# Log-sum-exp over heads: loads of two rows per partition, two heads on TensorE, hand-ordered issue and tapered last loads

## The chip, the cores and the metric

The kernel runs on one core of a Trainium2 chip. The metric is the device time of one execution in microseconds.

The time that is measured is about 1.9 us longer than the span that the profile shows (347.34 us against 345.5 us). Positions "at 331 us" below are in the span.

## The reference

```python
B, S, D, H = 8, 2048, 2048, 8            # x: (8, 2048, 2048) f32, bias: (8, 256) f32
x_heads = x.reshape(B, S, H, 256).transpose(0, 2, 1, 3) + bias[None, :, None, :]
x_tiled = np.repeat(x_heads, 2, axis=2)  # every row's result appears twice
mx  = x_tiled.max(axis=-1, keepdims=True)
lse = mx.squeeze(-1) + np.log(np.exp(x_tiled - mx).sum(axis=-1))   # (8, 8, 4096)
```

For each row and each of 8 heads, the kernel needs the log of the sum of exp(x + bias) over 256 columns. The kernels skip the maximum and compute log(sum(exp(x) * exp(bias))). The input is 134.2 MB, the output 1 MB. Each input element is read once, so the work is a stream: load, exp, weighted sum.

## The kernel before

A tile is 128 rows of 2048 columns, 1 MB, one row (8 KB) per partition. Seven heads go ScalarE (exp in place) then VectorE (multiply with exp(bias) and sum, one instruction per head, plus a second one that reads the sum out). The eighth head goes TensorE (bias row plus x by an identity matrix, in bf16) then ScalarE (exp with a sum).

```python
N_TTR_HEADS = 7
XIN_BUFS = 8
# ... constants: ident, ident_bf, ones_bf, brow (bias), w_rep = exp(bias) on 128 partitions ...
for b in range(B):
    for sblk in range(nsblk):                                   # 16 tiles per batch
        xt = xin.tile([P, D], mybir.dt.float32, name="xt")
        nc.sync.dma_start(out=xt, in_=x[b, s0 : s0 + P, :])      # 1 MB, 8 KB per partition
        for h in range(n_ttr, H):                                # the eighth head
            nc.tensor.matmul(ps, lhsT=ones_bf[0:1, :], rhs=b_hi, start=True, stop=False)
            nc.tensor.matmul(ps, lhsT=ident_bf[:, :], rhs=x_hi, start=False, stop=True)
            nc.scalar.activation(out=ps, in_=ps, func=ACT.Exp,
                                 accum_out=R[:, b, h, sblk : sblk + 1])
        nc.scalar.activation(out=xt[:, 0 : n_ttr * Dh], in_=xt[:, 0 : n_ttr * Dh], func=ACT.Exp)
        for h in range(n_ttr):                                   # seven heads
            nc.vector.tensor_tensor_reduce(out=junk, in0=xt[:, sl], in1=w_rep[:, sl],
                scale=1.0, scalar=0.0, op0=ALU.mult, op1=ALU.add,
                accum_out=R[:, b, h, sblk : sblk + 1])
    # ... per batch: transpose R (TensorE), Ln with each value written twice (ScalarE), store ...
```

The softmax here doesn't subtract the row's maximum and nothing guards it: scores larger than these inputs give would overflow.

## Time and profile before

| | before |
|---|---|
| time, median of 3 | 347.34 us (347.29 to 347.41) |
| span of the profile | 345.5 us |
| busy: VectorE / ScalarE / TensorE | 92% / 79% / 28% |
| load rate, 20 to 240 us | 421 GB/s |
| x has landed completely at | 336.71 us |
| from there to the end | 8.77 us |

The last two rows come from the trace's record of single DMA packets: 336.71 us is the end of the last packet of x, counted like every position here from the start of the profile's span. The prediction below has 336.9 us for it and 8.5 us for the rest, since it counts packets from a point 0.24 us earlier.

The page's slices of the kernel before (the span in 40 equal slices: mean busy share of the 16 DMA engines in tenths, and what they moved), and two lines of its DMA queues (packets, MB, share of 16 engines' span):

```profile
DMA  7999999999999999999999999999999999999700
GB/s 303 427 421 421 417 422 423 422 421 421 419 423 417 424 421 419 423 420 424 423 418 418 424 420 423 421 422 419 422 416 412 370 401 424 420 411 409 286 24 15
...
q1 hardware_dynamic: 18576, 134.36, 94.3%
q14 instruction: 23, 0.19, 0.1%
```

The DMA engines are busy in every slice from the 2nd to the 37th, at 409 to 427 GB/s but for a dip in slices 32 and 33 (268 to 285 us). Slice 39 (328 to 337 us) passes at 24 GB/s, about the rate of one DMA engine of 16 (the mean busy share of the 16 is 0.06 from 328 to 336 us, at 25 GB/s); the last slice holds the store of the results. Queue q14 is the fetch of instructions: 23 packets of 8 KB.

Groups of instructions of the kernel before (line, engine, operation, shapes, count | busy us, mean ns of one | idle before them and what ended it):

```profile
L131 DVE CUSTOM_DVE_ANT_0 junk<-xt,w_rep 128x256 f32<-128x256 f32 x896 | 316.3, 422 | 24.0 <-ACT xt L123 15.4
L123 ACT ACTIVATE xt<-xt 128x1792 f32<-128x1792 f32 x128 | 217.2, 1698 | 62.7 <-DMA xt<-in_x_dram 56.2
...
L112 PE MATMUL ps<-xt,ident_bf 128*128 128x256 bf16 x128 | 49.3, 385 | 21.4 <-DMA xt<-in_x_dram 21.3
L115 ACT ACTIVATE ps<-ps 128x256 f32<-128x256 f32 x128 | 47.2, 369 | 0.0
```

VectorE's 896 reductions start about 0.347 us apart (the 422 ns of one overlap the next), so 7 of them take 2.43 us. A megabyte arrives every 2.49 us at 421 GB/s. VectorE is nearly as busy as the DMA, but it is not what the others wait for, as the waits say (engine and tile <- what ended the wait: us in total, times, longest):

```profile
ACT xt L123 <- DMA xt<-in_x_dram: 56.2, 105, 3.7
DVE junk L131 <- ACT xt L123: 15.4, 23, 1.0
```

ScalarE, which with TensorE is the first to touch x, waits 105 times for x to land. Once x is there, the rest follows.

### The profile page before, as it was taken

How to read it: one execution, taken by the hardware profiler on the slowest of the kernel's cores; microseconds unless marked ns; L12 is line 12 of the kernel's file. 1: busy time of each engine (PE TensorE's matmuls, PEld its weight loads, DVE VectorE, ACT ScalarE, POOL GpSimd, SP SyncE). 2: the span in 40 equal slices, each digit the busy share in tenths (PEclk: the TensorE clock that was granted, in tenths of full speed). 3: DMA queues.
4: the chain of work that ended last, by engine and by line, in shares of the span. 5: the costliest groups of instructions: out<-in, count | busy, mean ns of one | idle time of the engine just before them, and what ended most of it. 6: DMA issues, size and time to landing. Idle time of an engine off the chain costs nothing. (4 is left out here: it accounts for less than half of the span.)

```text
span 345.5 us, 3541 instructions
## 1 busy us (share of the span) xinstructions
PE 95.0 (28%) x268; PEld 27.6 (8%) x268; DVE 316.6 (92%) x1793; ACT 272.4 (79%) x397; POOL 5.0 (1%) x15
## 2 busy tenths in 40 slices
PE   2423223223322323322332322232223232222220
PEld 0100000000000000000010000000000000000000
DVE  0899989899898998999989989899899998999985
ACT  4978878788787887878778878788777887878872
POOL 1000000000000000000000000000000000000000
DMA  7999999999999999999999999999999999999700
GB/s 303 427 421 421 417 422 423 422 421 421 419 423 417 424 421 419 423 420 424 423 418 418 424 420 423 421 422 419 422 416 412 370 401 424 420 411 409 286 24 15
DMA packets 18939, 135.50 MB, mean 392 GB/s; under 512 B 2177, under 2 KB 2305, under 8 KB 2529
## 3 DMA queue, kind: packets, MB, share of 16 engines
q1 hardware_dynamic: 18576, 134.36, 94.3%
q0 software_dynamic: 336, 0.92, 0.7%
q14 instruction: 23, 0.19, 0.1%
q8 instruction: 2, 0.03, 0.0%
q10 hardware_dynamic: 2, 0.01, 0.0%
HBM read 134.23 MB, written 1.05 MB: 392 GB/s over the span
## 5 line engine op out<-in xcount | busy, mean ns | idle before, releaser
L131 DVE CUSTOM_DVE_ANT_0 junk<-xt,w_rep 128x256 f32<-128x256 f32 x896 | 316.3, 422 | 24.0 <-ACT xt L123 15.4
L123 ACT ACTIVATE xt<-xt 128x1792 f32<-128x1792 f32 x128 | 217.2, 1698 | 62.7 <-DMA xt<-in_x_dram 56.2
L109 PE MATMUL ps<-brow,ones_bf 1*128 1x256 bf16 x128 | 46.9, 368 | 207.6 <-ACT ps L115 207.5
L131 DVE DVE_READ_ACCUMULATOR2_ANT R<- 128x1 f32 x896 | 74.8, 83 | 0.0
L112 PE MATMUL ps<-xt,ident_bf 128*128 128x256 bf16 x128 | 49.3, 385 | 21.4 <-DMA xt<-in_x_dram 21.3
L115 ACT ACTIVATE ps<-ps 128x256 f32<-128x256 f32 x128 | 47.2, 369 | 0.0
L112 PEld LDWEIGHTS <-ident_bf 128*128 128x128 bf16 x128 | 13.2, 104 | 245.2 <-issue 245.2
L115 ACT ACTIVATION_READ_ACCUMULATOR ps<-ps 128x1 f32 x128 | 23.5, 184 | 0.0
L109 PEld LDWEIGHTS <-ones_bf 1*128 1x128 bf16 x128 | 12.5, 98 | 45.6 <-issue 45.6
L152 ACT ACTIVATE res<-tps 128x256 f32<-128x256 f32 x8 | 3.1, 383 | 6.6 <-PE tps L143 6.6
L159 POOL DMA_DIRECT2D out_dram<-res x7 | 3.9, 562 | 295.9 <-ACT res L152 295.9
L143 PE MATMUL tps<-ident,R 128*128 128x128 f32 x8 | 3.6, 452 | 13.8 <-DVE R L131 13.8
L79 PE MATMUL psw<-brow,ones_bf 1*128 1x512 bf16 x4 | 2.4, 601 | 4.2 <-DMA brow<-in_bias_dram 2.4
L143 PEld LDWEIGHTS tps<-ident,R 128*128 128x128 f32 x8 | 1.4, 180 | 19.3 <-issue 15.8
L82 ACT ACTIVATE w_rep<-psw 128x512 f32<-128x512 f32 x4 | 2.3, 593 | 0.0
L50 ACT ACT_TABLE_LOAD x1 | 1.3, 1283 | 0.7 <-PEq L174 0.7
L63 DVE MEMSET ones_bf<- 1x128 bf16 x1 | 0.2, 165 | 0.8 <-PEq L174 0.8
L79 PEld LDWEIGHTS <-ones_bf 1*128 1x128 bf16 x4 | 0.5, 118 | 4.0 <-issue 3.0
masks.py:199 POOL TENSOR_SCALAR_AFFINE_SELECT ident<-ident 128x128 f32<-128x128 f32 x1 | 0.3, 285 | 0.0
masks.py:199 POOL TENSOR_SCALAR_AFFINE_SELECT ident_bf<-ident_bf 128x128 bf16<-128x128 bf16 x1 | 0.3, 285 | 0.0
masks.py:197 POOL MEMSET ident<- 128x128 f32 x1 | 0.2, 205 | 0.3 <-POOLq L174 0.3
masks.py:197 POOL MEMSET ident_bf<- 128x128 bf16 x1 | 0.2, 206 | 0.0
(4 smaller groups left out, 0.4 us busy)
## 6 DMA issues: line engine op xcount, KB each, us to landing
xt<-in_x_dram SPq DMA_DIRECT2D x128, 1024.0 KB, 16.4
out_dram<-res POOLq DMA_DIRECT2D x7, 128.0 KB, 5.8
out_dram<-res SPq DMA_DIRECT2D x1, 128.0 KB
brow<-in_bias_dram ACTq DMA_DIRECT2D x1, 8.0 KB
```

The lines of the kernel that those rows point to most:

```text
L50: nc.scalar.add_instruction(mybir.InstLoadActFuncSet(name=nc.get_next_instruction_name(), act_func_set_id=set_idx,))
L63: nc.vector.memset(ones_bf, 1.0)
L79: nc.tensor.matmul(psw, lhsT=ones_bf[0:1, :], rhs=b_hi_c, start=True, stop=True)
L82: nc.scalar.activation(out=w_rep[:, c * WCH : (c + 1) * WCH], in_=psw, func=ACT.Exp)
L109: nc.tensor.matmul(ps, lhsT=ones_bf[0:1, :], rhs=b_hi, start=True, stop=False)
L112: nc.tensor.matmul(ps, lhsT=ident_bf[:, :], rhs=x_hi, start=False, stop=True)
L115: nc.scalar.activation(out=ps, in_=ps, func=ACT.Exp, accum_out=R[:, b, h, sblk : sblk + 1],)
L123: nc.scalar.activation(out=xt[:, 0 : n_ttr * Dh], in_=xt[:, 0 : n_ttr * Dh], func=ACT.Exp,)
L131: nc.vector.tensor_tensor_reduce(out=junk, in0=xt[:, sl], in1=w_rep[:, sl], scale=1.0, scalar=0.0, op0=ALU.mult, op1=ALU.add, accum_out=R[ ...
L143: nc.tensor.transpose(out=ps, in_=R[:, b].rearrange("p h s -> p (h s)"), identity=ident)
L152: nc.scalar.activation(out=res, in_=ps_view, func=ACT.Ln)
L159: out_eng.dma_start(out=ov, in_=res.rearrange("p s e -> p (s e)"))
```

## The change

The change has four parts, and each has its own aim.

1. **2 MB loads, two rows per partition.** Each partition gets 16 KB in one piece, in place of 8 KB.
2. **Fixed buffers and hand-ordered issue.** Nine buffers of 2 MB and an order of issue written out by hand replace pools and a scheduler.
3. **Two heads by TensorE and ScalarE.** VectorE falls from 14 reductions per 2 MB to 12. The matmuls are fp32 now, so x is no longer cut to bf16 for these heads; the bias goes in as three bf16 parts.
4. **Tapering.** The last nine tiles come in pieces of 1 MB, then 0.5 MB, then down to 256 columns, so that little work is left when the last byte lands. The last tile has its own small result path.

```diff
-N_TTR_HEADS = 7
-XIN_BUFS = 8
+K = 2
+NPE = 2
+NBUF = 9
+LAST_CUTS = [[0, 1024, 2048], [0, 512, 1024, 1536, 1792, 2048]]
...
+    xts = [sb.tile([P, K, D], F32, name=f"xt{i}") for i in range(NBUF)]
+    def pieces(t):
+        left = T - 1 - t
+        if left > 8:
+            return [(0, K, 0, D)]
+        if left > 3:
+            return [(k, k + 1, 0, D) for k in range(K)]
+        cuts = [[0, D // 2, D]] * K if left else LAST_CUTS
+        return [(k, k + 1, c0, c1) for k in range(K) for c0, c1 in zip(cuts[k], cuts[k][1:])]
+    def rows_of(t):
+        if t < T - 1:
+            return v.rearrange("(p k) d -> p k d", k=K)
+        return v.rearrange("(k p) d -> p k d", k=K)
+    order = tc.manual_schedule()
...
-                nc.tensor.matmul(ps, lhsT=ident_bf[:, :], rhs=x_hi, start=False, stop=True)
+            nc.tensor.matmul(p[:, 0:CPE], lhsT=ident, rhs=v, start=False, stop=True)   # fp32, 512 columns
...
+        for k0, k1, c0, c1 in pieces(t):
+            if c0 == 0:
+                got = add_bias([xt[:, k, 0:CPE] for k in range(k0, k1)])   # TensorE
+            exp_inplace(xt[:, k0:k1, w0:c1])                               # ScalarE
+            if c0 == 0:
+                for k in range(k0, k1):
+                    sum_biased(got[k - k0], lambda h: sum_at(k, h))        # ScalarE, 2 heads
+            for k in range(k0, k1):
+                for c in range(w0, c1, Dh):
+                    weigh(xt[:, k, c : c + Dh], c // Dh, sum_at(k, c // Dh))   # VectorE
+            if last and k0 == K - 1 and c0 == 0:
+                finish(b, ..., NBLK - 1, K, 0, 1, [nc.sync])     # Ln and 8 stores of the earlier blocks
+        if t + NBUF < T:
+            load(t + NBUF)
```

## The prediction

> **What bounds it now.** The loads. In the page's slices the DMA engines run at 417 to 427 GB/s nearly throughout; 134.2 MB of x at 421 GB/s is 319 us of the 345.5 us span. The waits agree: ScalarE waits 56 us, 105 times, for x to land, about 0.4 us per tile. VectorE is close behind: 7 reductions per tile start 0.347 us apart, 2.43 us of the 2.49 that 1 MB takes. The DMA queue waits for free buffers (259 us), but with 16.4 us of loads already queued: no starvation.
>
> **The end.** The DMA packet records show 15 engines finishing x at 326 to 327 us and one at 336.9; the slices fall to 24 GB/s, one engine's rate. I put the lag down to instruction fetch: 23 packets of 8 KB, most beside an x packet that took about 0.97 us instead of 0.31. After the last landing 8.5 us follow: exp 1.7, seven reductions, transpose 0.45, Ln 0.39, store and completion 3.
>
> **What the change does, per 2 MB (4.98 us today).**
> - VectorE: 12 reductions instead of 14, 4.16 us instead of 4.86.
> - ScalarE: one exp of 3072 (estimated from 1792 in 1.70 us: 2.7) plus four sums of 256 at 0.395, 4.3 us instead of 4.0; still below the DMA.
> - TensorE: two fp32 matmuls of 512 columns. The fp32 transpose of 128 takes 0.45 us, bf16 512 columns 0.60, so I estimate 1.9 us each; with the bias matmuls 4.3 to 5 us at today's speed.
> - Loads: 16 KB contiguous per partition, so packets should become 16 KB. Now 8 KB takes 309 ns at best (306 apart), 311 on average; [...] Halving the packets saves an estimated 2.5 to 5 ns per 8 KB, 2.5 to 5 us over 1024 packets per engine: 424 to 428 GB/s.
> - 18 MB of buffers instead of 8, fixed order: almost nothing, since the DMA does not starve.
> - Fetch lag: VectorE and TensorE instructions fall, ScalarE's rise from about 400 to 1120; I count 24 fetches instead of 23. The lag of 10 us stays and limits the gain.
> - Tail: the last piece is 256 columns, exp 0.3 and one reduction. But in-order ScalarE first waits for a 1.9 us matmul, then does Ln of earlier blocks and other pieces: I estimate 7.3 us instead of 8.5.
>
> **Sum.** On the critical path: load stream -4, tail -1.2, lag +0.4. Relieving VectorE is off it. 347.3 - 4.8 = 342.5 us, range 337.5 to 346.5. Faster by over 2%: 0.27; within: 0.70; slower: 0.03.
>
> **What would show it right.** x packets of 16 KB at 605 to 615 ns; steady slices of 424 to 428 GB/s; VectorE and ScalarE 80 to 87% busy, ScalarE's main wait still x landing; a last stretch of about 10 us at one engine's rate; last landing to end about 7.3 us.
>
> **What would make it wrong.** Packets stay 8 KB or bring no rate: 346. [...] The lag shrinks, or the dip at 265 to 285 us (370 and 401 GB/s) vanishes: below 338. TensorE becomes the pace: 348. The eight small stores at the end hold back the final ones: +1 to 2 us.

## The result, and the profile after

| | before | after |
|---|---|---|
| time, median | 347.35 us | 341.16 us (340.64 to 341.37, 4 runs) |
| span of the profile | 345.5 us | 339.2 us |
| busy: VectorE / ScalarE / TensorE | 92 / 79 / 28% | 80 / 87 / 70% |
| load rate, 20 to 240 us | 421 GB/s | 428 GB/s |
| last packet of x ends at | 336.71 us | 331.25 us |
| from there to the end | 8.77 us | 7.94 us |

The ratio is 0.982 (95% interval 0.9806 to 0.9834): within 2%. A ratio here is the mean time of one kernel's runs over that of the other's runs of the same rounds, so it is not quite the ratio of the medians that are quoted. Executions over 1.5% slower than the fastest of the same kernel are left out of the means. Of the 6.3 us that the span lost, 5.5 us lie before the last landing of x and 0.8 us after it.

Slices and DMA queues of the kernel after:

```profile
PEclk9999577587876587876589877698777698595756
DMA  8999999999999999999999999999999999988950
GB/s 300 427 433 428 424 429 430 429 429 426 425 430 430 423 427 424 436 423 428 425 435 417 431 425 428 430 428 425 429 432 424 428 418 420 422 346 277 309 209 19
...
q1 hardware_dynamic: 12800, 135.27, 95.6%
q14 instruction: 20, 0.16, 0.1%
```

From the 2nd to the 35th, the slices run at 417 to 436 GB/s. Then there is something new: four slices (36 to 39, 297 to 331 us) at 346, 277, 309 and 209 GB/s. The stretch at one DMA engine's rate (about 25 GB/s) is now only 2.5 us long, from 329 to 331.5 us, in place of nine.

Groups of instructions of the kernel after:

```profile
L170 DVE CUSTOM_DVE_ANT_0 junk<-xt,w_rep 128x256 f32<-128x256 f32 x768 | 271.0, 420 | 63.4 <-ACT xt L164 63.2
L150 PE MATMUL ps<-xt,ident 128*128 128x512 f32 x256 | 188.8, 872 | 84.0 <-DMA xt<-in_x_dram 83.5
L164 ACT ACTIVATE xt<-xt 128x3072 f32<-128x3072 f32 (+4 forms) x83 | 179.4, 2172 | 20.0 <-DMA xt<-in_x_dram 17.2
L156 ACT ACTIVATE ps<-ps 128x256 f32<-128x256 f32 x256 | 94.6, 370 | 14.0 <-PE ps L150 9.2
```

TensorE's clock is now granted at 0.77 on average, and its 256 fp32 records (two to a matmul) take 0.87 us each, so 1.75 us per matmul. ScalarE took over as the busiest engine, with 609 instructions in place of 397.

Waits of the engines in the kernel after, then those of the DMA queue (SPq), two lines of the kernel before (L92) and two of the kernel after (L90):

```profile
ACT xt L164 <- DMA xt<-in_x_dram: 17.2, 32, 1.6
DVE junk L170 <- ACT xt L164: 63.2, 66, 11.2
ACT ps L156 <- PE ps L150: 9.2, 6, 6.2
```

```profile
SPq L92 <- DVE R L131: 259.3, 120, 5.8
...
SPq L92 <- DMA xt<-in_x_dram: 1.3, 1, 1.3
...
SPq L90 <- DMA xt<-in_x_dram: 153.3, 59, 5.4
SPq L90 <- DVE R L170: 111.5, 51, 7.5
```

ScalarE's main wait is still the landing of x, but it fell from 56 us to 17 us, because ScalarE has more to do between landings. VectorE waits 63 us for ScalarE. The loads still wait for VectorE to free buffers (111.5 us), but e3 below shows that VectorE's busy time does not set the pace. In the queue there is a wait that hardly existed before: a load now waits for an older load to land (153.3 us, 59 times, where it was 1.3 us, once). In the trace the loads use eight semaphores in turn, and none starts before the transfer that had its semaphore last has landed: the eighth load is issued at 8.45 us, after the first one has landed at 8.43, although its buffer is free. At most eight loads are outstanding at any time in this trace, and in the taper these eight are small.

### The profile page after: what moved, and what is told of

It reads as the page before. It is cut to its first block, busy times and chain, and to the rows that moved or that the text cites. A ratio compares the mean times of both kernels' runs of the same rounds, so it can differ in the third digit from the quotient of the medians.

```text
span 339.2 us, 3449 instructions
## 1 busy us (share of the span) xinstructions
PE 238.3 (70%) x408; PEld 70.3 (21%) x408; DVE 271.8 (80%) x1538; ACT 295.0 (87%) x609; POOL 6.3 (2%) x14
## 4 chain that ended last, share of the span: by engine, by line
DMA 75%; ACT 17%; PE 4%; POOL 1%; issue 1%; DVE 0%; POOLq 0%; DVEq 0%; SPq 0%; ACTq 0%
DMA xt<-in_x_dram 72%; ACT xt L164 10%; ACT ps L156 6%; PE ps L150 3%; DMA b<-bparts 2%; DMA brow<-in_bias_dram 1%; PE ps L145 1%; ACT res L199 0%; DVE junk L170 0%; POOL brest L117 0%; POOL brest L119 0%; POOL bparts L116 0%; POOL bparts L118 0%; POOL b L122 0%; POOL bparts L120 0%
## 5 line engine op out<-in xcount | busy, mean ns | idle before, releaser
L170 DVE CUSTOM_DVE_ANT_0 junk<-xt,w_rep 128x256 f32<-128x256 f32 x768 | 271.0, 420 | 63.4 <-ACT xt L164 63.2
L150 PE MATMUL ps<-xt,ident 128*128 128x512 f32 x256 | 188.8, 872 | 84.0 <-DMA xt<-in_x_dram 83.5
L164 ACT ACTIVATE xt<-xt 128x3072 f32<-128x3072 f32 (+4 forms) x83 | 179.4, 2172 | 20.0 <-DMA xt<-in_x_dram 17.2
L156 ACT ACTIVATE ps<-ps 128x256 f32<-128x256 f32 x256 | 94.6, 370 | 14.0 <-PE ps L150 9.2
L150 PEld LDWEIGHTS ps<-xt,ident 128*128 128x128 f32 x256 | 58.0, 254 | 164.5 <-DMA xt<-in_x_dram 119.5
L170 DVE DVE_READ_ACCUMULATOR2_ANT R<- 128x1 f32 x756 | 61.9, 82 | 0.0
L145 PE MATMUL ps<-b,ones 3*128 3x512 bf16 x128 | 47.0, 439 | 6.5 <-DMA b<-bparts 6.5
L156 ACT ACTIVATION_READ_ACCUMULATOR ps<-ps 128x1 f32 x256 | 48.7, 190 | 0.0
L145 PEld LDWEIGHTS <-ones 3*128 3x128 bf16 x128 | 7.9, 95 | 83.1 <-issue 75.1
L126 PE MATMUL ps<-brow,ones 1*128 1x512 f32 x6 | 5.5, 1078 | 3.6 <-DMA brow<-in_bias_dram 3.6
```

What stands on the lines that cost most here:

```text
L126: nc.tensor.matmul(ps[i], lhsT=ones, rhs=brow[:, CPE + c : CPE + c + MM], start=True, stop=True,)
L145: nc.tensor.matmul(p[:, 0:CPE], lhsT=ones3, rhs=b3, start=True, stop=False)
L150: nc.tensor.matmul(p[:, 0:CPE], lhsT=ident, rhs=v, start=False, stop=True)
L156: nc.scalar.activation(out=p[:, c : c + Dh], in_=p[:, c : c + Dh], func=ACT.Exp, accum_out=dst(h),)
L164: nc.scalar.activation(out=v, in_=v, func=ACT.Exp)
L170: nc.vector.tensor_tensor_reduce(out=j, in0=v, in1=w_rep[:, c : c + Dh], scale=1.0, scalar=0.0, op0=ALU.mult, op1=ALU.add, accum_out=dst,)
```

## The experiments

Twelve kernels were run. In the table, "last x" is the end of the last packet of x in that run's profile, "rest" is from there to the end of the span.

| run | time, us | ratio to before | last x | rest |
|---|---|---|---|---|
| before | 347.3 | 1 | 336.71 | 8.77 |
| after | 341.16 | 0.982 | 331.25 | 7.94 |
| e1_8k_packets | 345.57 | 0.9954 | 335.42 | 7.80 |
| e2_pool_1024 | 341.45 | 0.9833 | 331.63 | 7.85 |
| e3_one_head_pe | 342.42 | 0.986 | 332.36 | 8.37 |
| e4_three_tiles_15 | 376.25 | 1.0818 | 364.94 | 7.75 |
| e5_pool_3072 | 462.7 | 1.3323 | 331.49 | 129 |
| e6_half_the_reductions | 335.03 | 0.9642 | 325.62 | 7.83 |
| e7_no_taper | 342.49 | 0.9864 | 329.32 | 11.55 |
| e8_before_16k_packets | 345.29 | 0.9942 | 332.30 | 11.19 |
| e9_before_16_bufs | 347.45 | 1.0004 | 336.84 | 8.76 |
| e10_half_red_pool_2048 | 339.6 | 0.9777 | 329.92 | 7.80 |
| e11_tail | 339.34 | 0.979 | 329.87 | 7.28 |
| e12_tail_32k_packets | 339.08 | 0.975 | 328.42 | 8.89 |

### e1: the change with packets of 8 KB

```diff
-        if t < T - 1:
-            return v.rearrange("(p k) d -> p k d", k=K)
         return v.rearrange("(k p) d -> p k d", k=K)
```

The place of a result in the output tile was swapped to match, so the result stays right.

> The changed kernel with the row order of its last tile used for all tiles: still 2 MB per load, but each partition gets two separate 8 KB rows, so packets are 8 KB as before; everything else stays. Theory A (packet size carries the load-stream part): steady slices fall from about 427.5 to about 421.5 GB/s, 4.4 us over 134.2 MB, so the time is about 345.5 us. Rival B (buffers, fixed order or 2 MB loads carry it): packets of 8 KB change nothing, about 341 us.

Measured: 345.57 us, and the last landing 4.17 us later. The steady stretch (windows of the run: stretch in us, its length, busy time and count of each engine, granted clock, DMA share, GB/s) is back at 421; the second line is the same stretch of the kernel after:

```profile
20.00:240.00 220.00, 163.34 (x274) 47.18 (x272) 183.66 (x1041) 198.41 (x400) 0.00 (x0) 0.72 1.01 421
```

```profile
20.00:240.00 220.00, 158.47 (x278) 47.62 (x277) 186.44 (x1056) 200.89 (x406) 0.00 (x0) 0.76 1.01 428
```

Theory A holds to within 0.1 us. The packet size, not the size of the load, the buffers or the order, carries 4.4 of the 6.2 us.

### e8: the same part alone, in the kernel before

```diff
-XIN_BUFS = 8
+XIN_BUFS = 6
...
-            xt = xin.tile([P, D], mybir.dt.float32, name="xt")
-            nc.sync.dma_start(out=xt, in_=x[b, s0 : s0 + P, :])
+            if k2 == 0:
+                xt2 = xin.tile([P, 2, D], mybir.dt.float32, name="xt2")
+                nc.sync.dma_start(out=xt2,
+                    in_=x[b, s0 : s0 + 2 * P, :].rearrange("(p k) d -> p k d", k=2))
+            xt = xt2[:, k2, :]
```

> The kernel before with one part of the change alone: loads of 2 MB, two consecutive rows per partition (16 KB packets), six buffers of 2 MB in place of eight of 1 MB; rows of the output come out permuted on purpose. Theory A (packet size is worth 4.4 us): about 343 us, steady slices near 427 GB/s. If the freeing of buffers in steps of 2 MB throttled the loads, it would be slower than that. Rival (fixed order and relieved VectorE are needed for the gain): 347 us.

Measured: 345.29 us. The stream gains what it should, since the last landing is 4.41 us earlier at 428 GB/s. But the rest after it grows by 2.42 us, to 11.19 us: the last load is 2 MB, so two tiles' worth of work is left when it lands, not one. More than half of the gain is given back at the end. This is what the tapering is for.

### e7: the change without tapering

```diff
-        if left > 8:
+        if left > 0:
             return [(0, K, 0, D)]
-        if left > 3: ... cuts ...
+        return [(k, k + 1, 0, D) for k in range(K)]
```

> The changed kernel with every load of 2 MB but the last two rows' (1 MB each), so no tapering. Estimate: the last landing comes about 0.9 us earlier (no packets under 8 KB), but ScalarE has up to 2 MB of work (4.4 us) queued when the last megabyte lands, so the stretch from last landing to end grows from 7.7 to 10 us or more: time about 343 us. Rival (tapering is worth nothing): 340.3 us.

Measured: 342.49 us. The last landing comes 1.93 us earlier, the rest grows by 3.61 us. Tapering costs stream time and gives more than that back at the end: 1.3 us net. Its packets are 8, 4, 2 and 1 KB, but how much of the 1.93 us these explain was not separated. The expectation had both signs right and both sizes too small.

### e3: one head on TensorE instead of two

```diff
-NPE = 2
+NPE = 1
```

> The changed kernel with one head on TensorE and ScalarE instead of two, so VectorE does 14 reductions per 2 MB again (4.86 us). Prediction's claim A (relieving VectorE is off the critical path): time near 341 us, plus about 1 us for 2 VectorE fetches more and 2 fewer elsewhere; at most 343. Rival B (VectorE's relief is what made the kernel faster): back to about 346 us, with VectorE near 93% busy and few waits for ScalarE.

Measured: 342.42 us, with VectorE 92% busy, exactly as in the kernel before. Relieving VectorE's arithmetic is therefore worth 1.3 us at most, and not because VectorE was the pace: the last landing itself moved by 1.11 us. The runs below explain that movement.

### e9: more buffers in the kernel before

```diff
-XIN_BUFS = 8
+XIN_BUFS = 16
```

> The kernel before with 16 buffers of 1 MB in place of 8 and nothing else changed. Prediction's claim (buffers are worth almost nothing; the dips of the slices after 260 us are only the fast DMA engines waiting for the late one): dips later or gone, time 346.5 to 347.4 us. Rival (lack of buffers starves the loads): 344 us or less.

Measured: 347.45 us, no change. But the dip at slices 32 and 33 is gone:

```profile
GB/s 305 429 419 423 422 421 424 417 424 420 421 423 417 423 422 417 425 421 420 425 418 424 421 421 419 422 424 422 421 421 420 419 423 422 421 419 422 168 24 15
```

So the dip never cost anything. Most DMA engines were ahead of one (in the kernel before, 15 are done with x at 326 to 327 us, the last at 336.71) and ran out of free buffers; with more buffers they run further ahead and then are done earlier (slice 38 passes at 168 GB/s in place of 286). The last landing (336.84 us) is set by the late engine, which does not care. In this run the loads no longer wait for VectorE to free buffers (259.3 us before) but for older loads to land (234.3 us, 110 times), so more than the eight outstanding loads seen in the trace of the kernel after were probably not tried. The same reading applies to the four low slices after the change: the other engines wait there, while the late one works on.

### e2: 1024 more instructions on GpSimd

Why is one DMA engine late? The prediction put it down to instruction fetch. In the trace of the kernel after, fetch packets are followed by a slow packet of x, and the records fall into two kinds:

```
                     fetch at us, took ns -> next x packet, took ns (a normal 16 KB packet: 611)
VectorE-like         53.81, 325 -> 1273    76.82, 325 -> 1273    153.13, 325 -> 1273   (12 in the run)
others               40.62, 309 ->  989    108.91, 318 -> 989    170.45, 309 ->  987
```

The first kind comes every 22 to 29 us, in which VectorE's records number 107 to 140, 127 on average; this is why it is called VectorE-like. It holds its DMA engine for about 0.31 + (1.27 - 0.61) = 0.97 us. In the kernel before, a single engine still moves x after 328 us, and the fetch at 332.12 us, 22.8 us after the last one of this kind, is followed on it by an x packet of 891 ns in place of 309: this kind does fall on the late engine.

```diff
+        for _ in range(16):
+            nc.gpsimd.memset(tiny, 0.0)      # [1, 1], once per tile x 16
```

> The changed kernel plus 1024 one-element memsets on the idle GpSimd, 16 per tile, which nothing waits for: 8 more instruction fetches of 8 KB. Theory A (one DMA engine carries all instruction fetches and sets the last landing; a fetch costs it 0.66 to 1 us): fetch packets rise from 20 to about 28 and the time by 5 to 8 us, to about 347 us, with a longer end at one engine's rate. Rival B (the late engine is late for another reason, or the fetches spread over the 16 engines): time within 1 us of 341.2.

Measured: 341.45 us, with the last landing 0.38 us later, although the fetches rose from 20 to 28:

```profile
q14 instruction: 28, 0.23, 0.2%
```

Theory A as it was put fell: a fetch is not a fetch. Either fetches do not matter at all, or they are spread over the 16 engines, or GpSimd's go through another DMA engine than VectorE's. The last is theory A2: each compute engine's instructions come through a DMA engine of its own, and the one that serves VectorE is the late one, because VectorE has the most instructions (1627 records in the kernel after, ScalarE 696).

### e5: 3072 more instructions on GpSimd

The same edit with 48 memsets per tile.

> As the run with 1024 more GpSimd memsets, but with 3072 (48 per tile), so about 24 more fetches of 8 KB, more than VectorE's 12. That earlier run cost only 0.3 us for 8 fetches. Theory A2 (each compute engine's instructions are fetched through one DMA engine of its own; VectorE's is the late one, so GpSimd's fetches cost nothing until they outnumber VectorE's): GpSimd's DMA engine becomes the late one with about 25 fetches at 0.6 to 0.7 us, time 5 to 9 us longer, about 348 us. Rival B (fetches are not what makes one engine late): within 1.5 us of 341.3.

Measured: 462.7 us, but this decides nothing. The one-element memsets follow each other every 0.147 us (each is 89 ns long), so GpSimd alone needed 450 us for 3072 of them, and only 17 of its fetches came before the last landing, which stayed at 331.49 us. The run does give GpSimd's fetch a size: fetch packets of mostly 309 ns, each followed by an x packet of about 960 ns, so 0.31 + 0.35 = 0.66 us. Seventeen of these are 11.2 us, and VectorE's twelve at 0.97 us are 11.6 us. Under A2 nothing should have moved, so the experiment was too small for its own question.

### e6: half of VectorE's instructions for the same data

```diff
-                for c in range(w0, c1, Dh):
-                    weigh(xt[:, k, c : c + Dh], c // Dh, sum_at(k, c // Dh))
+                for c in range(w0, c1, 2 * Dh):
+                    e = min(c + 2 * Dh, c1)
+                    weigh(xt[:, k, c:e], c // Dh, sum_at(k, c // Dh))
```

The result is wrong: two heads are summed into one. (Not shown: a scratch tile twice as wide, and nine one-time presets of the result tiles on GpSimd.)

> The changed kernel with one VectorE reduction over 512 columns in place of two over 256: the same data, half the VectorE instructions (6 fetches fewer), on purpose a wrong result. Theory A (VectorE's fetches make one DMA engine late and set the last landing): last landing 3.5 to 5 us earlier, time about 337 us. Rival B: VectorE's busy time falls by at most a tenth and is not critical, so about 341 us.

Measured: 335.03 us, 6.1 us less, with the last landing 5.63 us earlier. Slices, the fetch queue and a group of this run:

```profile
GB/s 302 425 436 432 425 428 427 423 432 428 424 428 427 430 427 429 427 430 425 430 426 429 425 427 434 429 429 421 432 425 432 425 418 422 422 419 410 398 171 18
...
q14 instruction: 14, 0.11, 0.1%
...
L173 DVE CUSTOM_DVE_ANT_0 junk<-xt,w_rep 128x512 f32<-128x512 f32 x385 | 240.9, 686 | 87.6 <-ACT xt L166 79.9
```

VectorE is still busy with its reductions for 241 us (271 us before the edit), the steady rate is the same, and fetches fell from 20 to 14. Six fetches at 0.97 us would be 5.8 us. And the low slices near the end nearly vanish (419, 410, 398), which fits the reading that those engines had been waiting for the late one.

### e10: the same, with 2048 more instructions on GpSimd

```diff
+        for _ in range(32):
+            nc.gpsimd.memset(tiny, 0.0)
```

> The run with half the VectorE reductions (6 VectorE fetches, 335.0 us) plus 2048 one-element GpSimd memsets (16 more fetches, all before the last landing, since a memset takes 0.146 us and they end near 300 us). In the earlier traces a VectorE fetch held its DMA engine 0.97 us, a GpSimd one 0.66 us. Theory A2 (each compute engine has a DMA engine of its own for its fetches): GpSimd's becomes the late one, 16 x 0.66 = 10.6 against 5.8 us, so the last landing comes about 4.7 us later than at half the reductions, time about 339.5 us. Theory A1 (all fetches go through the same DMA engine): 10.6 us later, 345.6 us. Rival B (GpSimd's fetches do not hold up x at all): 335 us.

The fetch queue of this run (14 packets in e6):

```profile
q14 instruction: 31, 0.25, 0.2%
```

Measured: 339.6 us, against 339.5 expected under A2, 345.6 under A1 and 335 under B; the last landing moved by 4.30 us (4.7 expected). With VectorE's instructions halved, GpSimd's own fetches become the ones that set the end. This is what a DMA engine per compute engine predicts, and neither rival predicts it. Nor does a spread over the 16 engines: one fetch more on each would be about 0.66 us.

The trace does not record which of the 16 engines moved a packet, but its records let one infer it. A packet starts 3 or 4 ns before its predecessor on the same engine ends, and a 2 MB load is 8 packets and one of 4 bytes on each engine, so a search can join the packets into 16 chains. In e10, from 14 to 275 us, all 14 GpSimd fetches fall on one chain, the one that had moved least of x (412.5 times 16 KB), and all 5 of VectorE's kind on another (420); the rest had 421.5 to 427.5. In the kernel after, from 27 to 270 us, all 10 fetches of VectorE's kind fall on one chain, again the last (380.5, the others 393.5 to 397.5). In e2, e5 and e6 the search splits VectorE's kind over two chains (in e5 GpSimd's too), but no chain of e2 or e5 holds fetches of both; the packets of e8, e11 and the kernel before could not be joined cleanly.

### e4: sparing one DMA engine

```diff
+        if t in (14, 30, 46):
+            for p0, p1 in ((0, 120), (120, P)):
+                nc.sync.dma_start(out=xts[t % NBUF][p0:p1], in_=rows_of(t)[p0:p1])
+            return
```

The edit was meant to give one DMA engine less of x than the others. That a load split this way does so was the author's assumption, on which the figures of theories A and A' rest; no trace of this case shows it.

> The changed kernel with three of the 55 full loads (tiles 14, 30, 46) split into 120 and 8 partitions; [...] Theory A (one engine is behind by about 15 us, and it is the highest): [...] the last landing comes about 13 us earlier, time about 328 us. Theory A' (one engine, but not the highest): [...] about +1 us, 342 us. Rival B (no single engine is behind): about 341 to 342 us.

Measured: 376.25 us, the median of four runs (one of them, 380.68 us, was slow and is left out of the ratio; the fast three are 374.62 to 376.57 us). Both theories about the late engine are untouched by it, since the split loads themselves are slow. In the stretch of the second one the engines were busy and moved half as much:

```profile
160.00:170.00 10.00, 2.35 (x6) 0.61 (x6) 5.54 (x32) 4.36 (x9) 0.00 (x0) 0.75 1.01 206
```

Three such tiles cost 35 us. Why the split loads run at half rate was not found out. As a way to spare one engine it is useless.

### e11: another order in the last row

Timeline of ScalarE in the kernel after, around the last landing at 331.25 us (start us, us, engine, line, operation, tiles, count, idle before):

```profile
330.88 1.05 ACT L164 ACTIVATE xt<-xt 128x1024 f32<-128x1024 f32 x1
331.83 0.38 ACT L156 ACTIVATE ps<-ps 128x256 f32<-128x256 f32 x1
...
332.35 0.37 ACT L156 ACTIVATE ps<-ps 128x256 f32<-128x256 f32 x1
...
332.72 0.58 ACT L199 ACTIVATE res<-tps 56x512 f32<-56x512 f32 x1
333.20 1.75 ACT L164 ACTIVATE xt<-xt 128x512 f32<-128x512 f32 x4
334.85 0.36 ACT L199 ACTIVATE res<-tps 8x256 f32<-8x256 f32 x1
336.48 0.37 ACT L199 ACTIVATE res<-tps 8x256 f32<-8x256 f32 x1 [1.28 <-PE tps L186]
```

When the last piece has landed, ScalarE still does the sums of the TensorE heads, the Ln of the earlier blocks, and only then the four last exps that VectorE waits for.

```diff
-        if left > 3:
+        if left > 0:
             return [(k, k + 1, 0, D) for k in range(K)]
-            if c0 == 0:
+            late = last and k0 == K - 1
+            if c1 == D if late else c0 == 0:          # last row: the TensorE sums come last
                 ... sum_biased ...
-            if last and k0 == K - 1 and c0 == 0:
+            if late and c0 == D // 4:                 # Ln of earlier blocks after the first exp
```

> A version meant to beat both: whole rows instead of half rows in the three tiles before the last, and in the last row the exps go first, then the Ln of the earlier blocks, the TensorE sums last (a third result buffer, so that the last store need not wait). If ScalarE's in-order queue after the last landing is what the tail consists of: last landing about 0.4 us earlier, the stretch after it about 1.8 us shorter, time 339 us. If the tail is set elsewhere (stores, VectorE): 341 us.

Measured: 339.34 us (338.93 to 340.96, ratio 0.979, interval 0.9769 to 0.981, which overlaps that of the change). The last landing came 1.38 us earlier, more than expected; the half-row loads are gone, which is probably why. The rest shrank by 0.66 us where 1.8 was expected: ScalarE was busy without a gap from well before the last landing to 333.7 us, so reordering moves its work about but removes none of it. A small gain, not clearly told from none.

### e12: packets of 32 KB

If 8 KB packets take 313.9 ns and 16 KB packets 307.75 ns per 8 KB (means of the records of 20 to 240 us), and a packet costs a fixed time beside its bytes, that time is 2 x (313.9 - 307.75) = 12.4 ns, and the bytes alone take 301.5 ns. This can be tested by doubling once more.

```diff
-NBUF = 9
+NBUF = 8
+QB = 5                                        # first five batches: four rows per partition
...
+    xtp = [sb.tile([P, 2 * K, D], F32, name=f"xt{i}") for i in range(NBUF // 2)]
...
+                nc.sync.dma_start(out=xtp[t // 2 % (NBUF // 2)],
+                                  in_=v.rearrange("(p q) d -> p q d", q=2 * K))     # 4 MB
```

> The tail version with, for the first five of the eight batches, loads of 4 MB with four rows (32 KB) per partition, four such buffers in place of nine of 2 MB; the output stays right. Packets of 8 and 16 KB took 313.9 and 307.75 ns per 8 KB on average, so a packet costs about 12.4 ns beside its bytes (estimate) and 32 KB packets would take 304.65: 3.1 ns less for 640 of the 1024 units of 8 KB per DMA engine, 2 us. If packets grow to 32 KB and the model holds: last landing about 328 us, time about 337.3 us. If packets stay at 16 KB or gain nothing more: 339.3 us. If 4 MB lumps leave ScalarE behind or buffers short: above 340 us.

Measured: packets of 32 KB, 304.59 ns per 8 KB on average where 304.65 was expected. The last landing came 1.45 us before that of e11, at 328.42 us. The steady stretch:

```profile
20.00:200.00 180.00, 131.50 (x239) 40.47 (x238) 150.57 (x855) 165.21 (x337) 0.00 (x0) 0.79 1.00 430
```

The ratio is 0.975 (0.9732 to 0.9768), clear of that of the change: this version, with e11's order, beats both kernels, by 2.5% and about 0.7%, with a right result. Its median of 339.08 us is above the 337.3 expected: the rest after the last landing was 8.89 us, and in its timeline ScalarE waits 0.95 us for a TensorE matmul until 328.4 us. Against e11 the medians differ by only 0.26 us and the ranges overlap.

## Why the prediction was right or wrong

The predicted time was 342.5 us (337.5 to 346.5), the measured one 341.16 us, so the change of -6.2 us was forecast as -4.8. The parts did less well than the sum, and that the sum came so close is in part luck: two things it did not price, fewer VectorE fetches (up to 2.98 us earlier, e8 to e7) and the stream time of the taper (1.93 us later, e7), partly cancelled.

- **Load stream, -4 us predicted: right, in mechanism and size.** Packets became 16 KB, at 611 to 625 ns from 20 us on but for those beside a fetch, and the steady rate rose from 421 to 428 GB/s. Undoing that alone (e1) costs 4.4 us. (The saving per 8 KB was 6.2 ns, from 313.9 to 307.75, where the author's estimate was 2.5 to 5.) The three packet sizes extrapolate to 301.5 ns per 8 KB for endless packets (an estimate from 313.9 and 307.75 ns, which e12's 304.59 fits).
- **Fetch lag, +0.4 us predicted: wrong.** The step "I count 24 fetches instead of 23. The lag of 10 us stays" failed twice. The count was a slip: ScalarE has 609 instructions, not 1120, since 2 MB need four sums, not eight; the page shows 20 fetches. And the total is the wrong thing to count. Only the compute engine whose fetches cost most in sum mattered in these runs: VectorE in the kernel after (six fetches fewer saved 6.1 us in e6, eight more of GpSimd cost 0.3 us in e2), GpSimd in e10 (17 fetch packets more than e6, 4.6 us). VectorE's records fell from 1930 to 1627, and the fetches of its kind before the last landing from 15 to 12. One such fetch holds a DMA engine 0.97 us by the records. Giving two back with the second head (e3, 14 fetches) moved the last landing by 1.1 us, taking six away (e6) by 5.6 us. So "Relieving VectorE is off it" is right for VectorE's time and wrong for VectorE's instructions.
- **Tail, -1.2 us predicted, -0.83 measured.** The mechanism was right: ScalarE's in-order queue (the four last exps start at 333.20 us, 1.95 us after the last landing, behind two sums and an Ln). But it hides two large terms: 16 KB loads alone lengthen the rest by 2.4 us (e8), and the taper shortens it by 3.6 us (e7) at the price of 1.9 us of stream time. The prediction saw neither, and did not price the smaller packets of the taper.
- **"A last stretch of about 10 us at one engine's rate": wrong.** It was 2.5 us. The lag is still there, but the other engines no longer race ahead to the end: they are in part idle between 297 and 331 us (mean busy share of the 16: 0.79). That at most eight loads are outstanding, and small ones in the taper, is read from the trace (between 290 and 331 us the queue waits 25.8 us, 18 times, for an older load to land, and the loads use eight semaphores); that this is what keeps the other engines idle is argued from it. e11, which has larger last loads, keeps 422 GB/s up to 312 us and supports it.
- **Buffers and order "almost nothing": right for buffers** (e9, 0.04%). The hand-made order was not tested alone.
- **The dip at 265 to 285 us** was listed as something that might vanish and bring the time below 338. It vanished and brought nothing, because it was the wait of the fast engines for the late one (e9).
- **Busy shares** of 80 and 87% were as predicted. TensorE needed 1.75 us per fp32 matmul where 1.9 was estimated, and did not set the pace.

The landing can be walked through in steps, each being one run to the next:

| step | last x, us | rest, us |
|---|---|---|
| before | 336.71 | 8.77 |
| + 16 KB packets (e8) | -4.41 | +2.42 |
| + two heads, order, buffers, no taper (e7) | -2.98 | +0.36 |
| + taper (after) | +1.93 | -3.61 |
| after | 331.25 | 7.94 |

The packet records fit the second step's 2.98 us: before the last landing they hold 15 fetches of VectorE's kind in e8 and 12 in e7, and three at 0.97 us each are 2.9 us (an estimate from the records; e6 gave 5.6 us for six, but e3 only 1.1 us for two). Order and buffers changed in the same step, and the stores of results moved from GpSimd's queue to the sync queue; neither was tried alone.

## What to carry to other kernels

When a kernel is bound by its loads, look at the single DMA engine that finishes last, not at the mean rate: it fixed the end here, the dips of the others were harmless, and what slows it may be the instruction stream of a busy compute engine, so fewer and larger instructions can shorten a kernel whose arithmetic is not the limit (6.1 us of 341 in e6). Make each partition's contiguous piece long (8, 16 and 32 KB took 313.9, 307.75 and 304.6 ns per 8 KB here), but then cut the last loads small, or the work left after the last landing gives half the gain back (2.42 of 4.41 us in e8). Test a reading of idle slices by giving the idle part what it seems to lack; here twice the buffers changed the picture and not the time (347.45 us against 347.3).
